# A retuned stage of routing gates in a one-layer decoder kernel: buffers, order numbers and four early rows

## The chip, the cores and the metric

The kernel runs on one core of one Trainium2 chip. Its time is the device time of one execution in microseconds (us). The median of the three runs shown is 1644.31 us (1640.9 to 1646.19). The profiled execution took 1639.83 us; the time from its first to its last instruction, the span, is 1638.0 us. All times of the trace count from the span's start.

## The reference

One inference step of a one-layer decoder on 544 tokens (512 of a prompt, 8 sequences of 4), 1024 wide, fp32. The first half (a mixer with pooling and mLSTM heads) is finished before the part that changes. The second half is PEER, a product-key retrieval over 16384 experts of one neuron each:

```
def one(xb):                                             # a block of tokens
    q = (xb @ w_q).reshape(blk, PEER_HEADS, 2, HALF_KEY)
    s = jnp.einsum('nhpc,hpkc->nhpk', q, keys)
    sv, si = lax.top_k(s, TOPK)                          # 8 heads, 2 halves, 16 of 128 keys
    comb = sv[:, :, 0, :, None] + sv[:, :, 1, None, :]
    cidx = si[:, :, 0, :, None] * N_KEYS + si[:, :, 1, None, :]
    top, sel = lax.top_k(comb.reshape(..., 256), TOPK)
    eidx = jnp.take_along_axis(cidx.reshape(..., 256), sel, axis=-1)
    g = jax.nn.softmax(top, axis=-1)
    act = jax.nn.gelu(jnp.einsum('nd,nhkd->nhk', xb, u_tab[eidx]), approximate=False)
    return jnp.einsum('nhk,nhkd->nd', g * act, v_tab[eidx])
```

Each token uses 128 rows of u_tab and of v_tab (8 heads of 16).

## The kernel before

Tokens stand in five tiles: 0 to 3 of the prompt, 128 tokens each, and 4, the 32 sampled tokens. Two ways to compute PEER run side by side.

Tiles 1 to 3 (384 tokens) take the dense way, in 128 blocks of 128 experts. A **u block** (`uphase`) multiplies 128 rows of u_tab with all 384 tokens on TensorE: 24 matmuls of 384 columns into the bank pH, then one GELU on ScalarE into a tile act. Each factor is split into a high and a low part, so that three products replace an fp32 one: ScalarE writes the high part whi of a loaded weight tile raw, and VectorE or GpSimd the **low part** wlo = raw - whi. The first 16 matmuls of a u block need whi, the last 8 wlo. A **v block** (`vprep`, `ymm`) multiplies act by the block's gates (tile gr), splits the result into chi and clo, splits 128 rows of v_tab (tile vr), and adds 18 matmuls of 512 columns into the six banks Y. Activations of the first `AHEAD - RING` blocks are parked in DRAM (Ad) and reloaded as tile ar; the later ones stay in a ring of RING tiles.

Tiles 0 and 4 take the gathered way (`gathered`): for each of 160 steps (128 and 32) GpSimd's queue issues an indirect DMA that fetches one row of u_tab per token (128 rows of 4 KB), VectorE makes the dot product with the token (the tile dot), and then the same with v_tab rows, weighted and summed into y2. The rows pass through eight buffers rbuf, which share memory with the two halves of the tile stage.

The gates of the dense way are made in between. `topks` runs on VectorE tile by tile: the expert indices of the 16 chosen (tile f) by 16-fold one-hot products (eq, tr), and the softmax weights g. For tiles 1 to 3, three transposes on TensorE turn f and g. Then `gates_of` makes the gate rows, 8 tokens at a time, a **group**, 48 in all: VectorE writes a one-hot tile E and a tile P in two halves, TensorE multiplies them in 16 matmuls into two banks pg, ScalarE copies these into stage, and every four groups stage is written to DRAM (Gd), from which v blocks read their gates. GB is the number of buffers of P; E has one more.

All engines run in the order in which the program is written (a manual schedule). Where u blocks, top-k pieces and groups interleave is set by a small model while the program is built: the loop below `side, more, b, held = topks(), ...`. It keeps two clocks in us, `pe` and `dve`. Each piece of top-k yields its VectorE time, a group costs GRP there and PEG on TensorE, a u block PEU on TensorE and its low part LOU on VectorE; VectorE's clock starts at TOFF, the offset to TensorE's first u block after the sort. A group is placed on TensorE once its clock says that it is ready, else the next u block is. The first PLO low parts after the four that are placed earlier go to GpSimd, all later ones to VectorE. `WI.deep` is the number of blocks whose parts are written ahead of the one in use: the parts of block n + deep stand in the queues of ScalarE and VectorE before the GELU of block n. Of weight tiles (raw and vr together) four are in memory at a time.

When the groups are placed, RES u blocks remain before the passage to v blocks. In it SP's queue issues, in this order, the reloads of act (ar), the gates of the first four v blocks (gr), the remaining weight tiles and the first v rows; each waits for its buffer. The gathered steps start in the last three u blocks, GPRE steps in each, with up to seven rows fetched ahead (`Ahead`, depth 7). The first coefficient's low part clo is on GpSimd, behind the gathers issued so far. Then the loop over v blocks runs: while b is below AHEAD - RING it has v blocks alone with GV gathered steps each, then one u block and one v block an iteration with `pace` steps, at last v blocks alone.

Of the kernel before, what the change touches and what calls it, by code (L numbers as in the profile page):

```python
# [8 lines left out]
F32 = mybir.dt.float32  # L9
# [25 lines left out]
NRAW = 4  # L35
NSP = 4
GORD = (3, 2, 1, 0)
AHEAD = 55
SPILL = AHEAD - RING
GB = 5  # L40
RES = 6
GPRE = 2
GRP = 2.65
LOU = 1.25
LOL = 2.50
PLO = 4
PEU = 4.25
PEG = 1.10
TOFF = 14.00
PEW = 0.50  # L50
LEAD = 4.00
PRE = (4, 7, 10, 13)
# [94 lines left out]
def body(tc, a, o, stop=None):  # L147
# [1083 lines left out]
    eid = {0: gat.tile([128, 128], I32, name="eid0"), 4: gat.tile([128, 32], I32, name="eid4")}  # L1231
    gcf = {0: gat.tile([128, 128], F32, name="gcf0"), 4: gat.tile([128, 32], F32, name="gcf4")}
    nstep = {0: 128, 4: 32}
    heads_of = [slice(8 * t, 8 * t + 8) for t in range(4)] + [slice(32, 34)]

    def ranks():
        ex = grl.tile([128, HS, 16], F32, name="ex")
        tmp = keep.tile([128, 6, HS, 16], F32, name="rtmp", tag="ylo")
        ri, ci, cf_, rf, t1, t2 = (tmp[:, k] for k in range(6))
        ri, ci = ri.bitcast(I32), ci.bitcast(I32)  # L1240
        nc.vector.tensor_tensor(ex, top, top[:, :, 0:1].to_broadcast([128, HS, 16]), op=ALU.subtract)
        hk = "q h k -> q k h"
        si = sel.bitcast(I32)
        nc.vector.tensor_scalar(ri, si, 3, None, op0=ALU.arith_shift_right)
        nc.vector.tensor_copy(rf, ri)
        nc.vector.tensor_scalar(ci, si, 7, None, op0=ALU.bitwise_and)
        nc.vector.tensor_copy(cf_, ci)
        yield 3.0
# [9 lines left out]
        yield 5.5  # L1258
        return ex, sx, ii, jj

    def exps(ex):
# [6 lines left out]
    def topk(t, ex, sx, ii, jj):  # L1268
# [10 lines left out]
        for p, src in ((0, ii), (1, jj)):  # L1279
            eq = grl.tile([128, 16 * K], F16, name="eq", tag="eq", bufs=1)  # L1280
            e4 = eq.rearrange("q (b k h) -> q b k h", b=16, k=16)
            nc.vector.tensor_tensor(e4, src[:, None, :, hs].to_broadcast([128, 16, 16, nh]),
                                    io16[:, :, 0:K].rearrange(v, k=16), op=ALU.is_equal)
            nc.vector.tensor_tensor(e4, e4, ib[:, p, None, :, :].rearrange("q o b h -> q b o h").to_broadcast([128, 16, 16, nh]),
                                    op=ALU.mult)
            tr = grl.tile([128, 8 * K], F16, name="tr", tag="tr", bufs=1)
            nc.vector.tensor_tensor(tr, eq[:, 0:8 * K], eq[:, 8 * K:], op=ALU.add)
            for w in (4, 2):
                nc.vector.tensor_tensor(tr[:, 0:w * K], tr[:, 0:w * K], tr[:, w * K:2 * w * K], op=ALU.add)
            nc.vector.tensor_tensor(f[:, p, :], tr[:, 0:K], tr[:, K:2 * K], op=ALU.add)  # L1290
            if t == TORD[0] and p:
                sums(ex, sx)
            yield 4.2 if K == 128 else 1.6
# [4 lines left out]
        if t in eid:  # L1298
            nc.vector.scalar_tensor_tensor(eid[t], f[:, 0, :], 128.0, f[:, 1, :], op0=ALU.mult, op1=ALU.add)
        else:  # L1300
            turned.append((t, f, g))

    GSC = 2.0 ** 15
    stage = [None]
# [18 lines left out]
    def gates_of(ring):  # L1323
# [28 lines left out]

        todo = [(t, n0) for t in (1, 2, 3) for n0 in range(0, 128, W)]
        E = one_hot(*todo[0])
        for j, (t, n0) in enumerate(todo):
            nE = one_hot(*todo[j + 1]) if j + 1 < len(todo) else None
            P = ring.tile([128, 2, R, 128, RUN], F16, name="P", tag="P", bufs=GB)
            for k in (1, 0):
# [5 lines left out]
    def topks():  # L1364
# [3 lines left out]
        for t in TORD:  # L1368
# [1 line left out]
            for _ in last:  # L1370
                pass
            if turned:
                yield 1.6
                last = gates_in()
                yield next(last)
                next(last)
# [5 lines left out]
        yield from gates_of(ring)  # L1382


    WI.deep = 3
    side, more, b, held = topks(), True, next(nu), False
    pe, dve, wait, freed, lo_at = 0.0, TOFF, [], [], [0.0] * PLO
    while more or wait:
# [13 lines left out]
        elif b < AHEAD - RES and not (wait and wait[0][0] <= pe + PEW):  # L1402
# [2 lines left out]
            b += 1  # L1405
            pe = max(pe, lo_at.pop(0) - LOL) + PEU
            if b + WI.deep > ub + PLO:
                dve = max(dve, pe - PEU) + LOU
                lo_at.append(dve + 0.2)
        else:  # L1410
            ready, run_it = wait.pop(0)
            run_it()
            pe = max(pe, ready) + PEG
            freed.append(pe + 0.2)
    WI.deep = 2
    grx.close()
    gpx.close()
    gs.close()
# [5 lines left out]
    utab, vtab = a["u_tab"], a["v_tab"]  # L1424
    rbuf = [keep.tile([128, 4, D], F32, name="rbuf", tag=k) for k in ("yhi", "ylo")]
    rn = [0]

    def gathered():
        for t in (0, 4):
            n = nstep[t]  # L1430
            u = utok if t == 0 else usam
            dots = vp.tile([128, n], F32, name=f"dot{t}")
            cf = vp.tile([128, n], F32, name=f"cf{t}")
            CH = 16

            def row_of(tab, k):
                g = rbuf[rn[0] % 8 // 4][:, rn[0] % 4, :]
                rn[0] += 1
                nc.gpsimd.indirect_dma_start(out=g, out_offset=None, in_=tab,  # L1439
                                             in_offset=bass.IndirectOffsetOnAxis(ap=eid[t][:, k:k + 1], axis=0))  # L1440
                return g
            work = [("u", k) for k in range(CH)]
            for c0 in range(0, n, CH):
                work += [("c", c0)]
                for k in range(c0, c0 + CH):
                    work += [("v", k)] + ([("u", k + CH)] if k + CH < n else [])
            seq = [w for w in work if w[0] != "c"]
            q = Ahead(lambda i: row_of(utab if seq[i][0] == "u" else vtab, seq[i][1]), len(seq), 7)
            for kind, k in work:
                if kind == "u":  # L1450
                    g = q.get()
                    nc.vector.scalar_tensor_tensor(g, g, 1.0, u, op0=ALU.mult, op1=ALU.mult,  # L1452
                                                   accum_out=dots[:, k:k + 1])
                    yield 1
                elif kind == "c":
                    s = slice(k, k + CH)
                    nc.scalar.activation(cf[:, s], dots[:, s], AF.Gelu)
# [152 lines left out]
    while todo_u < AHEAD:  # L1610
# [6 lines left out]
            vprep(2 - AHEAD + todo_u)  # L1617
        uphase(todo_u)
        todo_u += 1
    done = 3 * GPRE  # L1620
    spent = float(done)
    pace = (320 + 1 - done - GV * (AHEAD - RING) - GV2 * (RING - GEND)) / (NB - AHEAD)
    ends, early = None, 0
    for b in range(NB - 1):
        if todo_u < NB and todo_u - b <= RING:
# [12 lines left out]
        if b < NB - LASTB:  # L1638
            for t in range(NDT):
                ymm(b, t)  # L1640
        want = min(320, int(spent))
        steps(gg, want - done)
        done = want
        if todo_u == NB and done >= 264 and FWAIT in fin and ends is None:
# [109 lines left out]
```

## Time and profile before

| | |
|---|---|
| median of 3 runs | 1644.31 us (1640.9 to 1646.19) |
| profiled execution | 1639.83 us, span 1638.0 us |
| TensorE busy (PE, matmuls) | 1548.3 us, 95% |
| VectorE busy (DVE) | 1349.4 us, 82% |
| ScalarE busy (ACT) | 639.6 us, 39% |
| GpSimd busy (POOL) | 698.2 us, 43% |
| bytes moved by DMA | 454.93 MB, mean 278 GB/s |

PE is TensorE, DVE VectorE, ACT ScalarE, POOL GpSimd, SP the engine that issues loads; SPq, ACTq and POOLq are their DMA issues. PEclk is the clock that TensorE was granted, 1.00 being 2.4 GHz and half of it 1.2 GHz. A span on GpSimd is rough. Matmuls overlap: one that is listed with 0.34 us starts 0.17 us after the one before it, so distances between starts are read, not durations. The part that the change touches lies between about 500 and 950 us: top-k to 591, groups to 738, the passage, and v blocks alone to 948. The rows below are of that part.

### The profile page before, as it was taken

The page shows a single profiled execution, that of the slowest core. Times are in us where ns is not written, and L with a number is a line of the kernel's source. Part 1 is how long each engine was busy: PE and PEld are TensorE (multiplying, and loading weights), DVE is VectorE, ACT ScalarE, POOL GpSimd, SP SyncE. Part 2 cuts the span into 40 slices and gives each one's busy share as a digit, 9 for nine tenths or more (in the row PEclk, how much of TensorE's full clock was granted, in tenths as well). Part 3 has the DMA queues.
Part 4 walks back from the last instruction along what each step waited for, and adds up shares of the span by engine and source line. Part 5 has one row for each costly group of instructions (what it writes and reads, how often), then busy time and mean ns, then how long its engine had stood idle before and what let it go on. Part 6 is the DMA issues. An engine that isn't in the chain of part 4 may idle for free.

```text
span 1638.0 us, 25202 instructions
## 1 busy us (share of the span) xinstructions
PE 1548.3 (95%) x9293; PEld 1378.1 (84%) x9293; DVE 1349.4 (82%) x2737; ACT 639.6 (39%) x999; POOL 698.2 (43%) x518
## 2 busy tenths in 40 slices
PE   5999998896999999998999999999999999999994
PEld 3888886676999989998788799999999999999873
DVE  6634468698999899994788789899889898989986
ACT  4322223555534345563333333333333333333343
POOL 2433333466551000004233356656565665566615
PEclk9999999998999999999999999999999999999997
DMA  9544456544344548769999989999999999999981
GB/s 346 179 145 155 151 150 186 196 170 132 111 142 151 186 165 290 283 267 350 374 369 381 357 311 378 378 367 369 367 379 381 353 370 376 375 366 367 388 282 68
DMA packets 180847, 454.93 MB, mean 278 GB/s; under 512 B 23216, under 2 KB 84016, under 8 KB 179060
## 3 DMA queue, kind: packets, MB, share of 16 engines
q1 hardware_dynamic: 119736, 246.70, 44.1%
q0 software_dynamic: 46080, 167.79, 27.0%
q10 hardware_dynamic: 14908, 38.84, 6.2%
q8 instruction: 73, 1.20, 0.3%
q14 instruction: 50, 0.41, 0.1%
HBM read 412.74 MB, written 40.53 MB: 277 GB/s over the span
## 4 chain that ended last, share of the span: by engine, by line
PE 72%; DVE 14%; DMA 7%; ACT 3%; issue 2%; POOL 1%; SPq 0%; ACTq 0%; DVEq 0%; POOLq 0%
PE pH L162 29%; PE Y L162 24%; PE bk L162 10%; PE tb L162 4%; DMA gr<-Gd 3%; PE pg L162 3%; DVE wlo L447 2%; PE pm L162 1%; DMA vr<-in_v_tab_dram 1%; DMA wm<-in_w_mod_r_dram 1%; PE tb L166 1%; DMA rbuf<-in_u_tab_dram,eid 1%; DVE ost L251 1%; ACT whi L445 1%; DVE x L987 1%
## 5 line engine op out<-in xcount | busy, mean ns | idle before, releaser
L1439 POOL DMA_INDIRECT rbuf<-in_u_tab_dram,eid x160 | 212.1, 1326 | 424.3 <-ACT stage L1347 235.4
L162 PE MATMUL pH<-u2hi,whi 128*128 128x384 f32 x992 | 338.1, 341 | 0.8 <-ACT act L1194 0.8
L162 PE MATMUL pH<-u2lo,whi 128*128 128x384 f32 x992 | 335.2, 338 | 0.0
L1439 POOL DMA_INDIRECT rbuf<-in_v_tab_dram,eid x160 | 237.0, 1481 | 178.2 <-DVE y L1464 125.5
L445 ACT ACTIVATE whi<-raw 128x1024 fp32r<-128x1024 f32 (+1 forms) x193 | 202.8, 1054 | 143.6 <-issue 96.5
L445 ACT ACTIVATE whi<-vr 128x1024 fp32r<-128x1024 f32 x128 | 135.6, 1059 | 300.5 <-PE Y L162 233.0
L162 PE MATMUL Y<-whi,chi 128*128 128x512 f32 x768 | 240.7, 392 | 5.4 <-ACT chi L1505 5.4
L162 PE MATMUL Y<-whi,clo 128*128 128x512 f32 x768 | 241.0, 393 | 2.3 <-DVE clo L1506 1.2
L162 PE MATMUL Y<-wlo,chi 128*128 128x512 f32 x768 | 239.4, 390 | 0.0
L447 POOL TENSOR_TENSOR wlo<-raw,whi 128x1024 fp32r<-128x1024 f32 (+2 forms) x65 | 152.0, 2347 | 160.3 <-ACT whi L445 158.9
L447 DVE TENSOR_TENSOR wlo<-vr,whi 128x1024 fp32r<-128x1024 f32 x128 | 156.6, 1223 | 75.8 <-ACT whi L445 69.0
L1464 DVE SCALAR_TENSOR_TENSOR y<-rbuf,cf,y 128x1024 f32<-128x1024 f32 x158 | 202.7, 1283 | 0.9
L162 PE MATMUL pH<-u2hi,wlo 128*128 128x384 f32 x992 | 194.4, 337 | 0.0
L162 PEld LDWEIGHTS pH<-u2hi,whi 128*128 128x128 f32 x992 | 186.9, 188 | 4.1 <-ACT act L1194 1.1
L162 PEld LDWEIGHTS pH<-u2lo,whi 128*128 128x128 f32 x992 | 186.9, 188 | 2.8
L447 DVE TENSOR_TENSOR wlo<-raw,whi 128x1024 fp32r<-128x1024 f32 (+1 forms) x132 | 160.3, 1217 | 34.0 <-ACT whi L445 25.3
L162 PEld LDWEIGHTS pH<-u2hi,wlo 128*128 128x128 f32 x992 | 175.8, 188 | 0.0
L162 PEld LDWEIGHTS Y<-whi,clo 128*128 128x128 f32 x768 | 144.2, 189 | 36.6 <-DVE clo L1506 5.0
L162 PEld LDWEIGHTS Y<-whi,chi 128*128 128x128 f32 x768 | 143.4, 188 | 32.9 <-ACT chi L1505 7.0
L162 PEld LDWEIGHTS Y<-wlo,chi 128*128 128x128 f32 x768 | 144.9, 189 | 30.4
L1452 DVE SCALAR_TENSOR_TENSOR rbuf<-rbuf,utok 128x1024 f32<-128x1024 f32 x128 | 156.0, 1221 | 1.6 <-DMA rbuf<-in_u_tab_dram,eid 1.6
L1194 ACT ACTIVATE act<-pH 128x384 f32<-128x384 f32 x124 | 60.8, 490 | 132.6 <-PE pH L162 128.7
(402 smaller groups left out, 2401.7 us busy)
## 6 DMA issues: line engine op xcount, KB each, us to landing
raw<-in_u_b_dram SPq DMA_DIRECT2D x128, 512.0 KB
vr<-in_v_tab_dram SPq DMA_DIRECT2D x128, 512.0 KB
wm<-in_w_mod_r_dram SPq DMA_DIRECT2D x48, 512.0 KB
gr<-Gd SPq DMA_DIRECT2D x32, 768.0 KB
Gd<-stage ACTq DMA_DIRECT2D x9, 2048.0 KB
raw<-in_w_q_b_dram SPq DMA_DIRECT2D x32, 512.0 KB
raw<-in_w_in_b_dram SPq DMA_DIRECT2D x20, 512.0 KB
Ad<-act ACTq DMA_DIRECT2D x42, 192.0 KB
```

The lines of the kernel that those rows point to most:

```text
L162: nc.tensor.matmul(out, l, r, start=start, stop=stop, skip_group_check=True)
L166: nc.tensor.transpose(out, x, idn)
L251: nc.vector.bn_stats(st[:, i, :], x[:, 512 * i:512 * (i + 1)])
L445: nc.scalar.activation(hi, raw, AF.Copy)
L447: e.tensor_tensor(lo[:, d], raw[:, d], f32(hi[:, d]), op=ALU.subtract)
L987: e.tensor_tensor(x1[:, d], x1[:, d], l1b[:rows, d], op=ALU.add)
L1194: nc.scalar.activation(x, p[:, 0:ND], AF.Gelu)
L1439: nc.gpsimd.indirect_dma_start(out=g, out_offset=None, in_=tab, in_offset=bass.IndirectOffsetOnAxis(ap=eid[t][:, k:k + 1], axis=0))
L1452: nc.vector.scalar_tensor_tensor(g, g, 1.0, u, op0=ALU.mult, op1=ALU.mult, accum_out=dots[:, k:k + 1])
L1464: nc.vector.scalar_tensor_tensor(y2[t], g, cf[:, k:k + 1], y2[t], op0=ALU.mult, op1=ALU.add)
```

## The change

Constants: P has three buffers instead of five (GB) and E four instead of six; the memory holds four row tiles re instead. Six low parts go to GpSimd instead of four (PLO). 53 u blocks are placed ahead of the loop over v blocks instead of 55 (AHEAD), so 40 activations are parked instead of 42. One gathered step in each of the last three u blocks instead of two (GPRE). The model's costs are new (GRP, LOU, TOFF and the times that top-k's pieces yield), and it now reckons a low part's earliest start one u block earlier. `WI.deep` stays 2 all the time, where it was 3 during top-k and groups. The first four u rows of tile 0 are gathered into the tiles re at a place of the program between the groups, and their dots follow the last group; the gathered steps then begin with row 4, at first with four rows ahead instead of seven.

```
-AHEAD = 55
+AHEAD = 53
-GB = 5
+GB = 3
+EG = 4
-GPRE = 2
-GRP = 2.65
-LOU = 1.25
+GPRE = 1
+GRP = 2.40
+LOU = 1.15
-PLO = 4
+PLO = 6
-TOFF = 14.00
+TOFF = 19.00
...
+    def gather(g, tab, t, k):
+        nc.gpsimd.indirect_dma_start(out=g, out_offset=None, in_=tab,
+                                     in_offset=bass.IndirectOffsetOnAxis(ap=eid[t][:, k:k + 1], axis=0))
+        return g
+
+    def dot_u(g, t, k):
+        nc.vector.scalar_tensor_tensor(g, g, 1.0, utok if t == 0 else usam, op0=ALU.mult, op1=ALU.mult,
+                                       accum_out=dots[t][:, k:k + 1])
...
+            if (t, n0) == (3, 32):
+                for k in range(EG):
+                    rows_early.append(gather(ring.tile([128, D], F32, name="re", tag="re", bufs=EG), utab, 0, k))
...
-    WI.deep = 3
     side, more, b, held = topks(), True, next(nu), False
...
             if b + WI.deep > ub + PLO:
-                dve = max(dve, pe - PEU) + LOU
+                dve = max(dve, pe - 2 * PEU) + LOU
                 lo_at.append(dve + 0.2)
...
-    WI.deep = 2
+    for k, g in enumerate(rows_early):
+        dot_u(g, 0, k)
...
-            work = [("u", k) for k in range(CH)]
+            work = [("u", k) for k in range(len(rows_early) if t == 0 else 0, CH)]
...
+            if t == 0:
+                rowq.append(q)
+                q.depth = 4
...
+    rowq[0].depth = 7
-    done = 3 * GPRE
+    done, ngat = 3 * GPRE, 320 - EG
     spent = float(done)
-    pace = (320 + 1 - done - GV * (AHEAD - RING) - GV2 * (RING - GEND)) / (NB - AHEAD)
+    pace = (ngat + 1 - done - GV * (AHEAD - RING) - GV2 * (RING - GEND)) / (NB - AHEAD)
```

How the instructions move. On TensorE the u blocks between the sets of transposes and the first group were 11, 3, 4 and 4 and are now 11, 4, 3 and 5; between the 48 groups stood 23 u blocks, two groups after almost each, and now stand 20, with two or three groups in turn.

On VectorE, where top-k ends (gcf and eid are its last tiles) and the groups begin. Before:

```order
L447 TENSOR_TENSOR wlo<-raw,whi 128x1024
L1295 TENSOR_TENSOR gcf_5575<-ex,sx_5735 128x2x16
L1299 SCALAR_TENSOR_TENSOR eid_5573<-f_6361 128x32
L1332 TENSOR_TENSOR E<-iT_4392,io_4391 128x2048 x2
L1360 TENSOR_TENSOR P<-E,gp_4395 128x1024 x2
L1332 TENSOR_TENSOR E<-iT_4392,io_4391 128x2048
```

Now:

```order
L1298 TENSOR_TENSOR gcf_5575<-ex,sx_5765 128x2x16
L1302 SCALAR_TENSOR_TENSOR eid_5573<-f_6391 128x32
L1346 TENSOR_TENSOR E<-iT_4392,io_4391 128x2048
L448 TENSOR_TENSOR wlo<-raw,whi 128x1024
L1346 TENSOR_TENSOR E<-iT_4392,io_4391 128x2048
L1378 TENSOR_TENSOR P<-E,gp_4395 128x1024 x2
```

A low part stands between the first two E; from the start of top-k (the tile ex) to the first E there are 17 low parts, where 20 stood, and 21 instead of 23 between the first and the last E.

On GpSimd, from its last low parts to the first v rows of the gathered way. Before:

```order
L447 TENSOR_TENSOR wlo<-raw,whi 128x1024 x22
L1439 DMA rbuf<-in_u_tab_dram,eid_5572 128x1024 x10
L1506 TENSOR_TENSOR clo<-ar,chi 128x384
L1439 DMA rbuf<-in_u_tab_dram,eid_5572 128x1024 x6
L1439 DMA rbuf<-in_v_tab_dram,eid_5572 128x1024
```

Now:

```order
L448 TENSOR_TENSOR wlo<-raw,whi 128x1024 x24
L1309 DMA re<-in_u_tab_dram,eid_5572 128x1024 x4
L1309 DMA rbuf<-in_u_tab_dram,eid_5572 128x1024 x5
L1523 TENSOR_TENSOR clo<-ar,chi 128x384
L1309 DMA rbuf<-in_u_tab_dram,eid_5572 128x1024 x7
L1309 DMA rbuf<-in_v_tab_dram,eid_5572 128x1024
```

Ten gathers stood ahead of the first clo, now nine do, of which the four into re wait for nothing but the indices (eid); seven instead of six follow it.

On SP, the loads at the passage. Before:

```order
L420 DMA raw<-in_u_b_dram 128x1024 x50
L1491 DMA ar<-Ad 128x384 x5
L1477 DMA gr<-Gd 128x12x128
L420 DMA raw<-in_u_b_dram 128x1024 x3
L1483 DMA vr<-in_v_tab_dram 128x1024 x4
```

Now:

```order
L421 DMA raw<-in_u_b_dram 128x1024 x47
L1508 DMA ar<-Ad 128x384 x5
L421 DMA raw<-in_u_b_dram 128x1024
L1494 DMA gr<-Gd 128x12x128
L421 DMA raw<-in_u_b_dram 128x1024 x3
L1500 DMA vr<-in_v_tab_dram 128x1024 x4
```

One weight tile, that of the fifth of the last six u blocks, now stands behind the reloads ar.

## Rows read from the trace of the kernel before

**Rows 1.** Stretches: us, then each engine's busy us and instructions, PEclk, DMA share, GB/s.
```profile
560.00:590.00 30.00, 30.00 (x175) 29.96 (x174) 27.21 (x53) 10.88 (x14) 0.00 (x0) 1.00 0.47 147
...
738.40:767.90 29.50, 25.51 (x144) 24.86 (x143) 9.29 (x13) 7.07 (x12) 10.18 (x10) 1.00 1.02 376
...
790.60:944.00 153.40, 152.13 (x664) 124.26 (x665) 130.38 (x184) 57.60 (x77) 50.72 (x44) 1.00 1.03 368
...
944.00:1550.60 606.60, 606.60 (x3068) 554.59 (x3068) 541.40 (x682) 221.16 (x299) 370.36 (x253) 1.00 1.00 369
```
**Rows 2.** Chain of waits, 480 to 860 us: start us, us, what.
```profile
496.94 46.47 PE pH L162 x264
...
595.83 5.40 PE pH L162 x24
...
603.08 4.26 PE pH L162 x24
...
607.35 1.85 PE pg L162 x32
```
**Rows 3.** Chain of waits, 860 to 1638 us.
```profile
948.29 4.22 PE pH L162 x24
...
952.50 4.09 PE Y L162 x18
```
**Rows 4.** TensorE timeline: start us, us, what, [idle before it <- who ended it].
```profile
594.33 1.50 PE L162 MATMUL pg<-P,E 128*128 128x128 f16 x16 [3.65 <-DVE P L1360]
...
767.90 0.73 PE L162 MATMUL Y<-whi,chi 128*128 128x512 f32 x2 [3.22 <-ACT chi L1505]
...
769.60 1.22 PE L162 MATMUL Y<-whi,clo 128*128 128x512 f32 x2 [0.96 <-POOL clo L1506]
...
775.72 0.62 PE L162 MATMUL Y<-wlo,chi 128*128 128x512 f32 x2
...
789.64 0.73 PE L162 MATMUL Y<-whi,chi 128*128 128x512 f32 x2 [1.06 <-ACT chi L1505]
```
**Rows 5.** VectorE timeline, top-k and gate products.
```profile
502.19 1.23 DVE L1120 TENSOR_TENSOR scr<-scr 128x32 f32<-128x32 f32 x1
...
510.26 0.17 DVE L1120 TENSOR_TENSOR scr<-scr 128x32 f32<-128x32 f32 x1
...
541.31 1.23 DVE L447 TENSOR_TENSOR wlo<-raw,whi 128x1024 fp32r<-128x1024 f32 x1 [1.49 <-ACT whi L445]
...
571.40 1.22 DVE L447 TENSOR_TENSOR wlo<-raw,whi 128x1024 fp32r<-128x1024 f32 x1 [1.79 <-ACT whi L445]
...
590.72 2.35 DVE L1332 TENSOR_TENSOR E<-iT,io 128x2048 f16<-128x2048 f16 x2
...
727.80 1.22 DVE L447 TENSOR_TENSOR wlo<-raw,whi 128x1024 fp32r<-128x1024 f32 x1
728.94 1.22 DVE L1332 TENSOR_TENSOR E<-iT,io 128x2048 f16<-128x2048 f16 x1
730.08 1.28 DVE L1360 TENSOR_TENSOR P<-E,gp 128x1024 f16<-128x1024 f16 x2
731.28 1.21 DVE L1332 TENSOR_TENSOR E<-iT,io 128x2048 f16<-128x2048 f16 x1
```
**Rows 6.** ScalarE, then GpSimd timeline.
```profile
758.72 1.06 ACT L445 ACTIVATE whi<-raw 128x1024 fp32r<-128x1024 f32 x1 [7.17 <-DMA raw<-in_u_b_dram]
...
766.38 1.06 ACT L445 ACTIVATE whi<-vr 128x1024 fp32r<-128x1024 f32 x1 [6.22 <-DMA vr<-in_v_tab_dram]
...
498.60 4.78 POOL L447 TENSOR_TENSOR wlo<-raw,whi 128x1024 fp32r<-128x1024 f32 x2 [3.29 <-ACT whi L445]
...
738.74 1.16 POOL L1439 DMA_INDIRECT rbuf<-in_u_tab_dram,eid  x1 [235.36 <-ACT stage L1347]
...
752.85 1.53 POOL L1439 DMA_INDIRECT rbuf<-in_u_tab_dram,eid  x1 [9.23 <-DMA Gd<-stage]
```

More of the change, by code (lines that the diff above doesn't have):

```diff
@@ L1233, in body @@
     nstep = {0: 128, 4: 32}
+    dots = {0: gat.tile([128, 128], F32, name="dot0"), 4: gat.tile([128, 32], F32, name="dot4")}
+    rows_early = []
     heads_of = [slice(8 * t, 8 * t + 8) for t in range(4)] + [slice(32, 34)]
@@ L1247, in ranks @@
         nc.vector.tensor_copy(cf_, ci)
-        yield 3.0
+        yield 2.4
         ii = grl.tile([128, 16, HS], F16, name="ii")
@@ L1257, in ranks @@
         sx = grl.tile([128, HS], F32, name="sx2")
-        yield 5.5
+        yield 4.5
         return ex, sx, ii, jj
@@ L1292, in topk @@
                 sums(ex, sx)
-            yield 4.2 if K == 128 else 1.6
+            yield (4.5 + 0.4 * (1 - p) + (1.1 if t == TORD[0] and p else 0.0)) if K == 128 else 2.1
         g = gcf[t] if t in gcf else grl.tile([128, 128], F32, name="g", tag="g", bufs=2)
@@ L1301, in topk @@
             turned.append((t, f, g))
+    utab, vtab = a["u_tab"], a["v_tab"]
+    def gather(g, tab, t, k):
[5 more added lines that the diff above has]
+                                       accum_out=dots[t][:, k:k + 1])
     GSC = 2.0 ** 15
@@ L1354, in gates_of @@
         E = one_hot(*todo[0])
+        yield 1.2
         for j, (t, n0) in enumerate(todo):
+            if (t, n0) == (3, 32):
+                for k in range(EG):
+                    rows_early.append(gather(ring.tile([128, D], F32, name="re", tag="re", bufs=EG), utab, 0, k))
             nE = one_hot(*todo[j + 1]) if j + 1 < len(todo) else None
@@ L1372, in topks @@
             if turned:
-                yield 1.6
+                yield 1.0
                 last = gates_in()
@@ L1423, in body @@
     y2 = {t: vp.tile([128, D], F32, name=f"y2_{t}") for t in (0, 4)}
-    utab, vtab = a["u_tab"], a["v_tab"]
+    rowq = []
     rbuf = [keep.tile([128, 4, D], F32, name="rbuf", tag=k) for k in ("yhi", "ylo")]
@@ L1430, in gathered @@
             n = nstep[t]
-            u = utok if t == 0 else usam
-            dots = vp.tile([128, n], F32, name=f"dot{t}")
+            dot = dots[t]
             cf = vp.tile([128, n], F32, name=f"cf{t}")
@@ L1438, in row_of @@
                 rn[0] += 1
-                nc.gpsimd.indirect_dma_start(out=g, out_offset=None, in_=tab,
-                                             in_offset=bass.IndirectOffsetOnAxis(ap=eid[t][:, k:k + 1], axis=0))
-                return g
-            work = [("u", k) for k in range(CH)]
+                return gather(g, tab, t, k)
+            work = [("u", k) for k in range(len(rows_early) if t == 0 else 0, CH)]
             for c0 in range(0, n, CH):
@@ L1451, in gathered @@
                     g = q.get()
-                    nc.vector.scalar_tensor_tensor(g, g, 1.0, u, op0=ALU.mult, op1=ALU.mult,
-                                                   accum_out=dots[:, k:k + 1])
+                    dot_u(g, t, k)
                     yield 1
@@ L1456, in gathered @@
                     s = slice(k, k + CH)
-                    nc.scalar.activation(cf[:, s], dots[:, s], AF.Gelu)
+                    nc.scalar.activation(cf[:, s], dot[:, s], AF.Gelu)
                     nc.vector.tensor_tensor(cf[:, s], cf[:, s], gcf[t][:, s], op=ALU.mult)
@@ L1640, in body @@
                 ymm(b, t)
-        want = min(320, int(spent))
+        want = min(ngat, int(spent))
         steps(gg, want - done)
         done = want
-        if todo_u == NB and done >= 264 and FWAIT in fin and ends is None:
+        if todo_u == NB and done >= 264 - EG and FWAIT in fin and ends is None:
             nc.scalar.preload_act_table_set("natural_log_exp_and_others")
```

## The prediction

> **What bounds the kernel now.** I read the page's slices first, then a table of stretches, the chain of waits from 480 us on, and last the timelines of the engines where TensorE has gaps. TensorE is the bound: from 944 to 1551 us it is busy in every one of 606.6 us [rows 1], and the chain there is one u block of 4.22 us and one v block of 4.09 us in turn [rows 3]. No edit takes a product away, so time can come only from TensorE's gaps near the change. There are two places. At the first gate products TensorE waits 3.65 us for VectorE and the next u block takes 5.40 us instead of 4.26 [rows 2, 4]. At the passage from u blocks to v blocks it waits 3.22, 0.96 and 1.06 us, and the eight pairs of v products from 767.90 to 775.72 take 6.86 us beside the 0.96, where eight pairs at 4.09/9 take 3.64: 3.2 us lost at half clock [rows 3, 4]. I call 738.4 us, where the last gate products end, G: 594.33 + 1.50 + 5.40 + 22 u blocks at 4.26 + 47 groups at 0.925 (half of 1.85) [rows 2, 4]. From G the kernel has six u blocks (25.3 us) and 42 v blocks (171.8) until the loop's first u block at 948.29 [rows 3]; ideal would be 935.5, so the passage loses 12.8 us. All through it the DMA engines are full: 376, then 368 GB/s [rows 1].
>
> **Top-k on VectorE, up to the first gate products.** A group on VectorE costs 1.14 us for the one-hot E and 1.20 for both halves of P, a low part 1.14, each the distance between two starts [rows 5]. By the order, 17 low parts stand there instead of 20: -3.4 us (two went to GpSimd, one more comes later because two blocks are prepared ahead instead of three). That same line costs something: the low part of block n now follows the GELU of block n-3, not n-4, so it cannot start until TensorE has ended n-3 and about 1.5 us have passed on ScalarE. Walking down the order with TensorE at 4.22 us a block (46.47/11 [rows 2]) I get four waits of 0.4, 0.6, 3.05 and 2.7 us, against 1.49 and 1.79 before [rows 5]: +3.5. The first E stays at 590.8 (before 590.72 [rows 5]). But TensorE now has 23 u blocks ahead of the first gates instead of 22 and arrives at 496.94 + 23 x 4.22 + 1.0 for three sets of transposes = 595.0. The first group is ready after E, a low part, E and P: 590.8 + 3 x 1.14 + 1.20 = 595.4. The wait falls from 3.65 us to about 0.4, too short for the clock to fall: after the wait of 1.06 us at 789.64 the granted clock was 1.00 [rows 1, 4].
>
> GpSimd's two extra low parts are not free for VectorE. A 128x32 addition took 1.23 us at 502.19, until GpSimd's low parts were over, and 0.17 us at 510.26 with GpSimd idle [rows 5, 6]. Two more low parts there (2.39 us each, half of 4.78) could hold VectorE up to 4.8 us where they save 2.3. The Trainium skill, "SBUF — State Buffer", section "Who interferes with whom", says the two engines share a port pair that one of them locks for a whole instruction when a Vector instruction has two SBUF inputs; by it the edit would lose up to 2.5 us of VectorE, and the trace agrees (1.23 against 0.17 us). In the sum I take 0: GpSimd gets these blocks' high parts at about 507 and 511 us, and the waits of 3 us later in top-k, which TensorE's pace sets, swallow the delay. If nothing swallows it, the first E is 2.5 us late.
>
> **The gate stage.** With the new order 20 u blocks stand between 48 groups, by twos and threes, where 23 stood before. TensorE: 48 x 0.925 + 20 x 4.26 = 129.6 us. VectorE: 48 x 2.34 + 21 x 1.14 = 136.3 us. So VectorE becomes the bound: it ends at 590.8 + 136.3 = 727.1, the last products 0.93 later, 728.0 at the earliest. TensorE meets the third group of a triple before it is ready, nine times by 0.6 to 0.9 us; walking down the order, G comes at 729.0 to 730.4. I take 729.5. Two u blocks are still owed at this point: 2 x 4.21 = 8.4, so 737.9 against 738.4: **-0.5 us**, with ends of -2 (G at 728.0) and +3.5 (first E 2.5 late and another 1.5 lost). Three buffers instead of five let VectorE run three groups ahead; in the walk no E or P waits for a buffer.
>
> **The passage.** Before, ten gathers (0.52 MB each) were issued here ahead of the first coefficient's low part, four from G on and six from 752.85 on, when the last stage write landed [rows 6]. Behind them the loads starved: the sixth u block's weights were waited for until 758.72, the first v rows until 766.38 [rows 6], 28 us after G. Now four rows are fetched earlier (by the order they need only the indices, so from about 584 us on, beside a DMA share of 0.47 [rows 1]) and five gathers, not ten, stand ahead of that low part. That is 2.6 MB, or 7 us at 376 GB/s, less in front of the first v rows. Against it, the first load of the six blocks that used to go out earlier (the fifth) now stands behind the five reloads: 0.5 MB, 1.4 us. The dots of the four early rows (4 x 1.22 = 4.9 us on VectorE) lie beside u blocks whose low parts are needed only at G + 11 us: no cost. So the first v rows land at about G + 22 to 24 instead of G + 27.9, and TensorE's own u blocks, ending at G + 25.3, come last, with 0.7 us left for ScalarE's high part and coefficients and about 1.1 for GpSimd's low part. Gained: 3.22 - 0.7 = 2.5, and the 3.2 us of half clock if waits of 0.7 and 1.1 us leave the clock up: 5.7; some of the rest (1.06 at 789.64, later waits) goes too.
> A second way to the same term: in this phase DMA is as full as TensorE. Until the loop's first u block it now moves two v blocks less (0.52 + 0.2 + 0.2 MB each) and 5.4 gathers less (3 + 40 x 1.2 against 6 + 42 x 1.2 rows), 4.7 MB or 12.6 us at 370 GB/s, while TensorE has 8.2 us less to do there: 4.4 us of slack, and up to 2 more because the first gathers wait for a stage write that now goes out 4 us earlier before G. Bounds: 0 (the loads stay as late, relative to the u blocks) and -10 (only unavoidable waits stay). I take **-6.5 us**, near what the two ways give.
>
> **The rest.** 128 u blocks and 128 v blocks remain; the loop takes 3.42 rows an iteration against 3.49 (the pace line), so DMA has a little less to do in a stretch where TensorE waits for nothing. At the end the order differs by one row sum moved one block: 0 +- 0.5.
>
> **Sum.** -0.5 - 6.5 = -7.0 us on the profiled execution's 1639.83 us (span 1638.0): 1632.8. That execution is 4.5 us under the median of the three runs; on the median the same step gives 1644.31 - 7.0 = 1637.3.
>
> **Rivals.**
> (a) The gate stage takes back what the passage gives. VectorE is the bound there, and each 0.1 us on a group is 4.8 us; with the +3.5 end and only -3 at the passage the change is +0.5: 1644.8. For it: 136.3 against 129.6 us. Against: the wait of 3.65 us that goes was larger.
> (b) Slower: three buffers are too few. If in each of the 20 rounds P waits for a buffer that TensorE frees late, VectorE, the bound, never makes it up: at 0.7 us a round G is 14 us later, -0.5 + 14 - 6.5 = +7.0: 1651. It decides from 0.6 us a round on. For it: the groups now come in threes, the number of buffers. Against: during a u block of 4.26 us VectorE makes a low part and 1.3 groups, and three may be open.
> (c) The transfer is no earlier. The fifth of the six blocks, now loaded behind the reloads, lands as late as the sixth did (G + 20.3): TensorE waits 4.5 us for it at G + 16.8 and loses 3.2 at half clock, v blocks begin at G + 33.0, which against G + 29.5 plus 0.96 and 3.2 lost there is -0.7; with the gate term -1: 1643.
> (d) More than forecast: the passage gives -10 and the gates -2: 1632.
>
> **How the numbers follow.** Chances: the forecast 0.50, its own range 1633 to 1641; (d) 0.10; (a) 0.15; (c) 0.15; (b) 0.10. About 0.3% (4.9 us) is the least that a measurement of this kernel tells from no change. Faster by more: most of the forecast and (d), 0.54. Slower by more: (b) and a little of (a), 0.12. Same: 0.34. The range takes in (a), (c) and (d), and a scatter of the runs of 2 to 3 us: 1629 to 1646.
>
> **What would show it.** Right: TensorE's wait before the first gate products under 1 us; then several waits on P of under 1 us each and the last gate products near 729.5 us; early gathers on GpSimd near 584 us; the first v product about 26 us after G with no half clock behind it. Wrong: G after 733 us, P waiting on TensorE, a wait for the fifth block's load, or the first v product 29 us after G again.

## The result, and the profile after

The changed kernel takes 1658.09 us (median of five runs, 1655.38 to 1660.94); the kernel before, run beside it, 1646.19 (1640.9 to 1651.18). The ratio is 1.0073, 95% interval 1.0045 to 1.0101: 12 us slower, where 7 us faster was forecast and the range ended at 1646. The profiled execution is the one of 1658.09 us, span 1655.9 against 1638.0.

The gate stage went as forecast. The chain of the kernel after (start, us, what), the timeline of GpSimd, and that of TensorE with idle time and its releaser in brackets:

```profile
502.46 46.48 PE pH L163 x264
...
596.82 1.22 DVE E L1346
```
```profile
590.76 1.16 POOL L1309 DMA_INDIRECT re<-in_u_tab_dram,eid  x1 [70.96 <-DVE eid L1302]
```
```profile
601.57 1.08 PE L163 MATMUL pg<-P,E 128*128 128x128 f16 x16 [1.15 <-DVE P L1378]
...
733.93 2.01 PE L163 MATMUL pg<-P,E 128*128 128x128 f16 x32
```

The u blocks begin 5.5 us later than in [rows 2], before any line that the change touches; the same start lies at 501.9, 502.0 and 503.2 us in three profiled variants of the kernel before (e3, e8, e2 below). That is scatter, and I subtract it. From the first u block to the last gate products are 233.5 us (733.93 + 2.01 - 502.46) against 241.5; with two u blocks owed (8.4) the stage costs 0.5 us more than before, where -0.5 was forecast.

What the prediction said of GpSimd's two extra low parts shows too. GpSimd, then VectorE beside them:

```profile
513.20 2.40 POOL L448 TENSOR_TENSOR wlo<-raw,whi 128x1024 fp32r<-128x1024 f32 x1 [1.80 <-ACT whi L446]
517.41 2.40 POOL L448 TENSOR_TENSOR wlo<-raw,whi 128x1024 fp32r<-128x1024 f32 x1 [1.80 <-ACT whi L446]
```
```profile
514.72 0.93 DVE L1121 TENSOR_TENSOR scr<-scr 128x32 f32<-128x32 f32 x1
...
517.81 2.58 DVE L1244 TENSOR_TENSOR ex<-top 128x544 f32<-128x544 f32 x1
```

The first addition takes 0.17 us with GpSimd idle [rows 5], the second took 0.72 us in the kernel before: together 2.6 us lost on VectorE, where the kernel before lost 1.1 on one addition [rows 5]. The first E is only 0.5 us later than forecast, so the later waits swallowed most of it, as the sum had assumed.

The passage did not go as forecast. TensorE, ScalarE, VectorE and SyncE's DMA issues of the kernel after:

```profile
756.24 0.69 PE L163 MATMUL pH<-u2hi,whi 128*128 128x384 f32 x1 [3.42 <-ACT act L1195]
...
766.16 0.63 PE L163 MATMUL Y<-whi,chi 128*128 128x512 f32 x2
...
790.14 1.22 PE L163 MATMUL Y<-whi,chi 128*128 128x512 f32 x2 [6.49 <-ACT chi L1522]
```
```profile
754.76 1.06 ACT L446 ACTIVATE whi<-raw 128x1024 fp32r<-128x1024 f32 x1 [9.82 <-DMA raw<-in_u_b_dram]
...
763.70 1.06 ACT L446 ACTIVATE whi<-vr 128x1024 fp32r<-128x1024 f32 x1 [2.31 <-DMA vr<-in_v_tab_dram]
```
```profile
788.91 0.56 DVE L1519 TENSOR_TENSOR ar<-ar,gr 128x384 f32<-128x384 f32 x1 [10.11 <-DMA gr<-Gd]
```
```profile
735.97 2.54 SPq L1508 DMA_DIRECT2D ar<-Ad  x5
738.61 0.66 SPq L421 DMA_DIRECT2D raw<-in_u_b_dram  x1
744.21 0.37 SPq L1494 DMA_DIRECT2D gr<-Gd  x1
750.19 2.67 SPq L421 DMA_DIRECT2D raw<-in_u_b_dram  x3
757.10 11.23 SPq L1500 DMA_DIRECT2D vr<-in_v_tab_dram  x4
...
772.76 0.44 SPq L1494 DMA_DIRECT2D gr<-Gd  x1
```

The chain has the links between these rows, and the last line is that of the kernel before:

```profile
738.61 16.06 DMA raw<-in_u_b_dram
...
755.85 1.24 DVE wlo L448
757.10 6.52 DMA vr<-in_v_tab_dram
```
```profile
753.13 13.17 DMA vr<-in_v_tab_dram
```

The fifth u block's weights are issued behind the five reloads and land 16 us later, at 754.7. The first v rows wait for the load buffer that this block holds: they go out at 757.1, when its low part is done, and ScalarE takes them at 763.7. Counted from the last gate products (G), they go out at 21.2 us instead of 14.7, but are under way for 6.5 us instead of 13.2. The second gate rows (issued at 772.8) arrive at 788.9; around their issue GpSimd sends out seven gathers in a row. The last gather ahead of them, then the first and the last of the seven:

```profile
750.96 0.94 POOL L1309 DMA_INDIRECT rbuf<-in_u_tab_dram,eid  x1 [10.05 <-issue]
...
767.05 1.75 POOL L1309 DMA_INDIRECT rbuf<-in_u_tab_dram,eid  x1 [0.15 <-issue]
...
777.16 1.30 POOL L1309 DMA_INDIRECT rbuf<-in_u_tab_dram,eid  x1 [0.30 <-issue]
```

The table of stretches (us, busy us and instructions of PE, PEld, DVE, ACT, POOL, granted clock, DMA share, GB/s) shows what the transfers did meanwhile:

```profile
736.00:746.00 10.00, 10.00 (x59) 10.00 (x59) 5.21 (x8) 3.66 (x6) 4.00 (x4) 1.00 0.92 322
746.00:756.00 10.00, 6.82 (x39) 6.50 (x38) 0.15 (x1) 1.24 (x2) 0.94 (x1) 1.00 1.05 378
756.00:766.00 10.00, 9.76 (x48) 9.76 (x49) 6.26 (x8) 3.93 (x6) 0.74 (x1) 0.83 0.71 265
766.00:800.00 34.00, 27.35 (x110) 21.00 (x109) 22.77 (x34) 11.01 (x17) 13.45 (x12) 0.90 0.97 338
...
943.50:1550.00 606.50, 606.50 (x3038) 550.17 (x3037) 528.17 (x664) 219.98 (x297) 363.12 (x245) 1.00 0.99 360
```

Before, the engines moved 376 GB/s over these 30 us [rows 1] (335, 382 and 408 in three stretches of about 10); now they fall to 265 just when the v rows are due. Little has been issued that they could move: SyncE's queue issues nothing from 752.9 to 757.1, and GpSimd no gather from 751.9 to 767.05. And the last row holds the surprise: from 943.5 to 1550 us TensorE waits for nothing and its clock is whole, as in [rows 1], yet the DMA engines move 360 GB/s, not 369: everything runs slower. The chain says why:

```profile
943.62 4.22 PE pH L163 x24
947.84 4.17 PE Y L163 x18
```

A v block takes 4.17 us, not 4.09 [rows 3]. The mean distances between the starts of its 18 products (59 or 60 blocks from 1000 to 1500 us, ns):

```
before 232 231 227 227 227 227 227 227 227 227 227 227 227 227 227 227 227 227  sum 4090
after  232 228 230 233 241 232 231 232 228 230 233 241 233 231 232 228 230 227  sum 4170
```

Every block repeats its pattern, at the whole clock and without a wait; in the kernel after the distances recur every seven products. What differs is where operands lie. The row dots moved into the pool gat (640 bytes more in each partition), before everything that is allocated later, and out of the pool of the coefficients (512 bytes less ahead of them), so the coefficient tiles chi and clo now start 128 bytes later: at 64 bytes past a multiple of 256, before at 192 past one (all eight alike). The tiles whi and wlo, which stream past them, stay at 192.

The difference of the spans, stage by stage: start +5.5 (scatter); gate stage +0.5; from the last gate products to the loop's first u block 207.7 us against 209.9, with two v blocks (8.2) fewer, +6.0; 74 pairs of the loop at 0.086 us, +6.4; the end -0.5. Sum 17.9. These are one execution of each kernel. From the last gate products to the loop, other profiled executions of the old order took 209.2 us (e8 below) and, with slower v blocks, 213.0, 213.3 and 215.5 (e2, e3, e10), so the +6.0 is uncertain by some us; what the runs say of it stands with e1.

### The profile page after: what moved, and what is told of

The parts are those of the page before. It is cut to its first block, busy times and chain, and to the rows that moved or that the text cites. A ratio compares the mean times of both kernels' runs of the same rounds, so it can differ in the third digit from the quotient of the medians.

```text
span 1655.9 us, 25195 instructions
## 1 busy us (share of the span) xinstructions
PE 1565.8 (95%) x9293; PEld 1385.2 (84%) x9293; DVE 1348.0 (81%) x2735; ACT 638.7 (39%) x999; POOL 709.1 (43%) x520
## 4 chain that ended last, share of the span: by engine, by line
PE 67%; DVE 20%; DMA 6%; issue 3%; ACT 2%; POOL 1%; SPq 0%; ACTq 0%; DVEq 0%; POOLq 0%
PE Y L163 27%; PE pH L163 23%; PE bk L163 10%; PE tb L163 4%; DMA gr<-Gd 3%; DVE E L1346 3%; DVE wlo L448 3%; DVE P L1378 3%; DMA raw<-in_u_b_dram 1%; PE pm L163 1%; DMA wm<-in_w_mod_r_dram 1%; PE tb L167 1%; DVE ost L252 1%; DVE x L988 1%; ACT whi L446 1%
## 5 line engine op out<-in xcount | busy, mean ns | idle before, releaser
L163 PE MATMUL Y<-wlo,chi 128*128 128x512 f32 x768 | 243.9, 396 | 0.0
L448 POOL TENSOR_TENSOR wlo<-raw,whi 128x1024 fp32r<-128x1024 f32 (+2 forms) x67 | 157.0, 2352 | 163.7 <-ACT whi L446 162.3
L1314 DVE SCALAR_TENSOR_TENSOR rbuf<-rbuf,utok 128x1024 f32<-128x1024 f32 x124 | 151.2, 1220 | 0.0
```

What stands on the lines that cost most here:

```text
L163: nc.tensor.matmul(out, l, r, start=start, stop=stop, skip_group_check=True)
L448: e.tensor_tensor(lo[:, d], raw[:, d], f32(hi[:, d]), op=ALU.subtract)
L1314: nc.vector.scalar_tensor_tensor(g, g, 1.0, utok if t == 0 else usam, op0=ALU.mult, op1=ALU.mult, accum_out=dots[t][:, k:k + 1])
```

## Experiments: where the operands lie

**e1 and e2: the coefficient tiles moved, the order left as it is.**

```
-            cf = vp.tile([128, n], F32, name=f"cf{t}")
+            cf = vp.tile([128, n + 96], F32, name=f"cf{t}")[:, 0:n]     e1, of the kernel after
+            cf = vp.tile([128, n + 32], F32, name=f"cf{t}")[:, 0:n]     e2, of the kernel before
```


> The changed kernel, with the tile cf0 made 384 bytes longer a partition, so that the coefficient tiles chi and clo behind it start 384 bytes later: at 448 bytes past a multiple of 512 again, as in the kernel before (the change put them at 64 past one). Nothing else moves. Theory A (where the coefficient tiles lie sets the rate of the v products): a v block takes 4.09 us again instead of 4.17, 128 x 0.08 = 10 us less, about 1648. Theory B (the rate comes from the order: 53 blocks ahead, other buffers for v rows, gathers at other moments): v blocks stay at 4.17 and the time at 1658.

> The kernel before, with the tile cf0 made 128 bytes longer, so that chi and clo lie where the changed kernel has them (64 bytes past a multiple of 512). Order and everything else as before. Theory A: v blocks of 4.17 us instead of 4.09, about 1656, 10 us slower than before. Theory B: 4.09 and no change, 1646.

Measured: e1 1649.19 us, ratio to before 1.0003 (0.9985 to 1.0022); e2 1655.16, 1.0046 (1.0028 to 1.0065). The chains of e1 and of e2:

```profile
1404.98 4.09 PE Y L163 x18
```
```profile
1406.63 4.17 PE Y L162 x18
```

Theory A holds in both directions, B falls: the same order with the tiles moved back has the old rate, and the old order with the tiles moved has the new one, within a nanosecond (e2 repeats the pattern of "after" above). In e1's profile the loop is 6.4 us shorter than in the kernel after, the stretch ahead of it only 0.4. There the 40 faster v blocks wait for transfers instead: from the first v product to the loop e1 takes 176.9 us, where 40 x 4.09 are 163.6. By the runs, what the change does besides moving the tiles is worth +0.5 us (ratio 1.0003, -2.5 to +3.6 us), where -7.0 was forecast.

In e1 and e2 all that is allocated behind cf0 moves along, not the coefficients alone. e3 below settles that: there the time of a block follows the place of its own chi and clo.

**e3, e8, e10: other places.**

```
-        ch, cl = (vp.tile([128, ND], F32R, name="c" + k, tag="c" + k, bufs=CB) for k in ("hi", "lo"))
+        ch, cl = (vp.tile([128, ND + 16], F32R, ..., bufs=CB)[:, 0:ND] for k in ("hi", "lo"))     e3
+    keep.tile([128, 16], F32, name="padw")        e8, ahead of wst; cf0 longer by 192 bytes
+    hi, lo = (wst.tile([128, D + 16], F32R, name=k, tag=k, bufs=NSP)[:, 0:D] ...)                 e10
```


> The kernel before with each buffer of chi and of clo made 64 bytes longer (not used), so that the four buffers start at different places: chi at 448, 0, 64 and 128 bytes past a multiple of 512, clo at 192, 256, 320 and 384. Theory A: the v blocks no longer take one time; every fourth block has its own, between 4.0 and 4.2 us, and the block whose chi starts at 64 is slower than the one at 448. Theory B: all v blocks take 4.09.

> The kernel before with all load and split buffers (raw, whi, wlo) 64 bytes later, so that whi and wlo start at a multiple of 256 instead of 192 past one, and the coefficients kept at 192 past one. In v products whi and wlo stream past and the coefficients are the stationary operand; in u products whi and wlo are the stationary operand. Theory H (the place of the stationary operand alone decides): v blocks 4.09 us, and u blocks slower than 4.22. Theory I (the two operands' places against each other decide): v blocks at 4.20, like the pair 64 bytes apart the other way round, or at 4.13.

> The kernel before with each buffer of whi and wlo made 64 bytes longer (not used), so that the four start at 192, 0, 64 and 128 bytes past a multiple of 256, the coefficients kept at 192. By turns v blocks then have whi and wlo at 192 and 64, u blocks at 0 and 128. From e3 and e8: v blocks 4.09 with whi at 192 and 4.12 at 0, u blocks 4.22 at 192 and 4.19 at 0. Theory H (the stationary operand's place alone decides) fell with e8's v blocks. Theory J (each operand's place has its own price, and the prices add up): v blocks with whi at 64 take 4.15 to 4.18, u blocks at 0 take 4.19, and u blocks at 128 another time, 4.17 to 4.25. Theory I (only the distance of the two operands): v blocks with whi at 64 (coefficients 128 further) take 4.17, as in e3 with the coefficients 128 off.

The chains of e3, e8 and e10 in the loop, of one execution each:

```profile
1412.55 4.09 PE Y L162 x18
...
1420.86 4.13 PE Y L162 x18
...
1429.21 4.17 PE Y L162 x18
...
1437.60 4.20 PE Y L162 x18
```
```profile
1401.12 4.19 PE pH L162 x24
1405.32 4.12 PE Y L162 x18
```
```profile
1405.03 4.20 PE Y L162 x18
1409.23 4.20 PE pH L162 x24
1413.43 4.09 PE Y L162 x18
1417.52 4.19 PE pH L162 x24
```

In bytes past a multiple of 256, with e11 below (in e3 chi and clo of one block stand at the same place by this count):

```
whi, wlo  chi, clo   v block   u block
192       192        4.09      4.22     before, e1
192         0        4.13               e3
192        64        4.17      4.22     after, e2, e3
192       128        4.20               e3
  0       192        4.12      4.19     e8
 64       192        4.20               e10
128         -                  4.20     e10
  0         0        4.10      4.20     e11
```

Theory A's forecast for e3 holds: four times, in turn. H falls with e8: the coefficients stood where they are fast, and the v block still rose from 4.09 to 4.12. J and I each miss a row: J (prices add) forecast 4.15 to 4.18 for whi at 64 and 4.16 for e11; I (distance alone) would give 192/128 and 0/192, both 64 bytes apart by the same way round, one time, and they have 4.20 and 4.12. What is shown is that the places of both operands count, at 64-byte steps, by up to 2.6% of a block, and that the best of those tried has both at the same place. The place of whi alone does not set the u block either: with whi at 0 it has 4.19 in e8 and 4.20 in e11. Why stays open. The Trainium skill, "SBUF — State Buffer", section "Specifications (TRN2)", speaks of lines of 16 bytes; by it places that are all multiples of 64 would be alike, and here they are not (4.09 to 4.20 us).

## Experiments: the passage

**e4, e5, e6, e7: one hold-up taken away at a time**, all with e1's coefficient tiles.

```
+    WI.early = 3                     e4: the fifth u block's load ahead of the reloads
+    WI.load()
     aq.fill()
-GV = 1.20
+GV = 1.10                            e5: e4, and fewer rows beside v blocks alone
+        if AHEAD - todo_u == 2:      e6: e4, and the second gate rows ahead of the v rows
+            load_g(4)
-        if b % 4 == 0 and b:
+        if b % 4 == 0 and b > 4:
         if AHEAD - todo_u == 5:
+            vq.depth = 1             e7: e4, and the first v rows in a buffer of their own
+            vq.fill()
+            vq.depth = 3
-        r = wst.tile([128, D], F32, name="vr", tag="raw", bufs=NRAW)
+        r = (wst.tile([128, D], F32, name="vr", tag="raw", bufs=NRAW) if b else
+             vp.tile([128, D], F32, name="vr", tag="sq", bufs=1))
```


> The kernel of e1_after_shift, and besides the fifth of the last six u blocks has its weights' load issued before the five reloads of activations, as in the kernel before. Theory C (the passage lost its gain because that load stood behind the reloads): ScalarE's wait of 9.8 us for it and TensorE's of 3.4 us go, the v blocks begin 3 us earlier, and the time is 3 us under e1_after_shift's. Theory D (the DMA queues are full there, so that what is loaded earlier makes another load later, first the v rows or the second gate rows gr, for which TensorE waits 6.5 us): the wait of 3.4 us goes but later ones grow, and the time is within 1 us of e1_after_shift's.

> The kernel of e4_fifth_load_first with 1.1 gathered rows instead of 1.2 beside each v block that has no u block (40 of them; the four rows, 2.1 MB, come later, in the loop). Theory E (from the last gate products to the loop's first u block the kernel is bound by what the DMA engines move; 371 GB/s in e4 from 800 to 936 us): 2.1 MB at 371 GB/s is 5.7 us that the v blocks get, as far as TensorE waits or runs at half clock there (e4 needs 175.5 us from the first v product to the loop's first u block, where 40 x 4.09 are 163.6): u1 - v0 of 170 to 172 and 1643 to 1645. Theory F (TensorE waits there for single late transfers, not for the amount): no change, 1648; or slower, if the loop, where the DMA engines are at 0.99, cannot take four rows more.

> The kernel of e4_fifth_load_first with the second load of gate rows (gr for v blocks 4 to 7) issued ahead of the first v rows instead of behind the fifth. Theory F (a single late transfer): the wait for gr at the fifth v block (3.6 us in e4, 6.5 in the changed kernel, each with half clock behind it) goes, u1 - v0 falls from 175.5 to about 170, 1643 to 1645. Theory E (amount): another wait takes its place, and u1 - v0 stays within 1.5 us, 1648.

> The kernel of e4_fifth_load_first with the first v rows in a buffer of their own, loaded right behind the fifth u block's weights, instead of in one of the four load buffers that the u blocks still hold (in e4 the first v rows are issued at 752.3 us, 19 us after the last gate products, and the DMA engines are at 206 GB/s from 753 to 763). Theory G (the load buffers, not the DMA engines, hold the first v rows back, and the engines idle meanwhile): the first v product comes at once behind the u blocks, 25.3 to 26.5 us after the last gate products instead of 27.95, the engines move 300 GB/s or more all through, and the time falls by 2 to 5 us, to 1643 to 1646. Rival: later waits take it back, 1648.

Measured (v0 is the first v product's start behind the last gate products; then from v0 to the loop's first u block):

```
      time us   ratio to before (95%)       v0      to the loop
e1    1649.19   1.0003 (0.9985, 1.0022)     30.2    176.9
e4    1648.23   1.0005 (0.9989, 1.0021)     28.0    175.5
e5    1648.44   1.0008 (0.9991, 1.0026)     29.3    173.5
e6    1648.33   1.0004 (0.9987, 1.0021)     31.9    173.7
e7    1645.82   0.9991 (0.9971, 1.0012)     25.1    175.8
```

None can be told from before by its time; the times of 1643 to 1645 that E and F forecast for e5 and e6 did not come, e7's lies in G's range but not clear of noise. The profiles show why, TensorE's timeline of e4, of e6 and of e7:

```profile
761.31 0.73 PE L163 MATMUL Y<-whi,chi 128*128 128x512 f32 x2 [2.65 <-ACT chi L1522]
...
785.56 0.73 PE L163 MATMUL Y<-whi,chi 128*128 128x512 f32 x2 [3.58 <-ACT chi L1522]
```
```profile
767.74 1.22 PE L163 MATMUL Y<-whi,chi 128*128 128x512 f32 x2 [6.63 <-ACT chi L1522]
```
```profile
788.24 1.22 PE L163 MATMUL Y<-whi,chi 128*128 128x512 f32 x2 [4.99 <-ACT chi L1523]
```

In e4 the wait of 3.4 us for the fifth block is gone (C), but the first v rows and gr are waited for, as D said, and the engines fall to 206 GB/s from 753.4 to 763.4 us. The edit does more than put the fifth load back: with WI.early at 3, one weight tile more than in the kernel after goes out ahead of the first v rows (56 instead of 55), and these now wait for the buffer of the sixth block. The chain of e4:

```profile
735.78 14.08 DMA raw<-in_u_b_dram
...
751.04 1.24 DVE wlo L448
752.29 7.41 DMA vr<-in_v_tab_dram
```

So the v rows go out at G + 18.9 in e4 and at G + 21.3 in e5, not at 14.7 as in the kernel before; what the fifth load alone costs no run shows. In e6 the wait for gr is gone (F), but behind the load that now stands ahead of them the first v rows are under way for 9.2 us (7.4 in e4, 6.4 in e5), and v0 is 3.9 us later than in e4, 2.6 later than in e5. In e7 the first v product comes at once (G, whose 300 GB/s are nearly reached: 317, 385, 298 in three stretches of 10 us), and gr is waited for. In e5 the forecast of E, 170 to 172, is missed by 1.5 us, and v0 is later. Up to v0 e4 and e5 have the same loads, so 28.0 and 29.3 also show how far two executions differ. Each edit hands the wait to the next transfer in line.

**e9: e5, e6 and e7 together.** The lines of all three, as above.

> The kernel of e7_first_v_own_buffer with the edits of e5_fewer_rows (1.1 rows) and e6_second_gate_rows_early. In e7 the first v product comes at 25.1 us behind the last gate products, but the fifth v block waits 5.0 us for gr and u1 - v0 is 175.8 us; e5 and e6 had 173.5 to 173.7. Theory E and F together (amount and a single late transfer): u1 - v0 falls to 168 to 170, the first v product stays at 25 to 27 us, about 6 us under e7, 1639 to 1641 where before is at 1647. Rival (the DMA engines are full from 776 us on, so what is taken away in one place is given back in another): u1 - v0 of 173 or more, 1644 to 1646.

Measured: 1637.23 us, ratio 0.9932 (0.9908 to 0.9955); v0 at 25.1, then 168.9 us. TensorE's timeline of e9 has one wait of some size left, and the engines stay full where they fell before (stretches as above):

```profile
766.76 0.73 PE L163 MATMUL Y<-whi,chi 128*128 128x512 f32 x2 [2.77 <-ACT chi L1523]
```
```profile
755.00:765.00 10.00, 8.99 (x46) 7.93 (x45) 4.54 (x6) 1.96 (x3) 5.42 (x5) 1.00 1.08 366
```

E and F hold together: 11 us under e4, more than the sum of the three alone (2.4, 0 and 0). 1639 to 1641 was forecast beside 1647 for the kernel before, which took 1648.2 here. Whether two of the three would do was not tried. This version is faster than both kernels.

**e11 and e12: the best of both, and the passage without the change.** e11 is e9 with e8's line padw alone, so that all four tiles start at a multiple of 256; e12 is the kernel before with the three edits of e9.

> The kernel of e9_passage_together with all load, split and coefficient buffers 64 bytes later: whi, wlo, chi and clo all start at a multiple of 256. Measured so far: whi at 192 with coefficients at 0: v block 4.13; whi at 0 with coefficients at 192: 4.12; whi at 0: u block 4.19 instead of 4.22. Theory J (the two prices add up): v blocks of 4.16, 128 x 0.07 slower, less 124 x 0.026 for the u blocks: 5 to 6 us slower than e9, about 1643. Theory I (only the distance of the two counts): v blocks of 4.09 again, and the u blocks' 3.2 us are gained: about 1634.

> The kernel before, with the three edits of the passage that e9_passage_together has (1.1 rows instead of 1.2 beside a v block without a u block, the second gate rows ahead of the first v rows, the first v rows in a buffer of their own), but without the change itself: five buffers of gate rows, no early rows, ten gathers ahead of the first coefficient, 55 blocks ahead. Theory K (the change gives what was forecast, once its loads are not held up): this comes out 4 to 7 us over e9, 1642 to 1644. Theory L (the change's own part is worth nothing, the three edits are all): the same as e9, 1637 to 1639. Rival: with ten gathers ahead, the first v rows stay late and the edits give nothing, 1647.

Measured: e11 1635.71 us, 0.9939 (0.9918 to 0.996): no difference from e9. Its chain:

```profile
1403.80 4.10 PE Y L163 x18
1407.90 4.20 PE pH L163 x24
```

J falls (v blocks 4.10, not 4.16), and I's gain on the u blocks is half what it was in e8 (4.20). e12 1642.81, 0.9978 (0.996 to 0.9995): within K's forecast, 5.6 us over e9 by the medians and 7.6 by the ratios; the two intervals do not meet, but they leave the size open by some 5 us either way. L falls; the rival's 1647 too. e12's profile is of its slowest execution (1652.93 us, 10 over the median). In it the weights of the sixth of the last u blocks, issued among the ten gathers, land 24 us later, and TensorE waits 11.2 us for them, a wait that e9 does not have:

```profile
758.29 23.94 DMA raw<-in_u_b_dram
```

From the first v product on it loses nothing (171.8 us to the loop, 42 x 4.09). If its other executions lose the same there, this is where the change's fewer gathers pay; no profile of one shows it.

## Why the prediction was wrong

1. **The step that failed first is one that the sum did not have.** "No edit takes a product away, so time can come only from TensorE's gaps" and "The rest ... 0 +- 0.5" took 4.22 and 4.09 us a block as fixed. The v block became 4.17. Worth 6.4 us in the loop by the profiles; in all 8.9 us by the medians of e1 and the kernel after, 11.5 by their ratios. No view of before shows it; the addresses of the two programs would have shown that the tiles move, not what that costs.
2. **The passage, -6.5 us, gave nothing.** It was +6.0 by the two profiles; by the runs, gate stage and passage together are +0.5 us (e1, -2.5 to +3.6), so how far beyond nothing it went is not known. The failed sentence is "the first load of the six blocks ... now stands behind the five reloads: 0.5 MB, 1.4 us". I priced the load's own bytes. It landed 16 us after its issue, and the first v rows stood behind it, not only in the DMA queue but for its load buffer, so they went out 6.4 us later (G + 21.2 against 14.7). Against that they were under way for 6.5 us instead of 13.2, which fits the 7 us forecast for five gathers fewer, though no run takes these away alone. The two cancel. "The first v rows land at about G + 22 to 24": ScalarE took them at G + 27.8, before at G + 28.0 [rows 6]. e7 shows the link of the buffer: with a buffer of their own v0 is 25.1 instead of 30.2, where 26 was forecast. e4 shows that TensorE's wait goes when the load goes out earlier, and no more, since its v rows stand behind the sixth block instead. This is rival (c), given 0.15, with its wait (4.5 forecast, 3.42 measured); its price for gate and passage, -1 us, lies within e1's interval. The wait for the fifth block and the first v product 29 us after G (30.2) are two of the prediction's own signs of being wrong.
3. **The second way to the same term** counted 12.6 us of DMA time less and assumed that the engines stay full. They fell to 265 GB/s: SyncE stood at a load whose buffer was not free, GpSimd at the first coefficient, and the gathers that used to fill this stretch were gone.
4. **The wait of 6.49 us for gr was not foreseen.** Seven gathers now go out in a row behind the first coefficient's low part, around gr's issue, where six stood; before, TensorE's wait at that place was 1.06 us [rows 4]. That the gathers make gr late is argued, no run changes them alone; issuing gr earlier (e6 and e9) takes the wait away.
5. **What held.** The first E at 591.3 us less the scatter (590.8 forecast); the first gate products after a wait of 1.15 us (0.4 forecast, 3.65 before); early gathers at 585.3 less the scatter (584); three buffers are enough, so rival (b) falls: VectorE waits for no buffer of E or P, and the last gate products come at 730.4 less the scatter (729.5), not 14 us later. The two low parts on GpSimd cost VectorE 2.6 us, of which 0.5 at most reached the first E.
6. **The size of the idea may be right, its sum was not.** With the loads freed and the coefficients at the old place, the change is worth 5.6 to 7.6 us (e9 against e12); 7.0 was forecast. But both have three edits that the forecast did not know, and e9 has the fifth block's load ahead of the reloads again: that the number fits is partly luck.

## What to carry to other kernels

Compare the addresses of TensorE's operands when a change adds or moves a tile, even a small one that no product reads: a block whose products all take a little longer, without a wait and at full clock, points there. Before moving a load behind others, ask not what its bytes cost but which buffer it fills, and what is issued only when that buffer comes free. Ask apart when a transfer is issued and how long it is under way: here the first became 6.4 us later and the second 6.7 us shorter, and nothing was gained. Where a chain of transfers is late, removing one wait may show nothing in the time until the next ones go too, as in e5 and e6, so try the edits together before dropping them.

## What was not expected of the hardware

The 128x512 products of a v block have starts 227 ns apart (but for the first two of a block, 232 and 231) where stationary and moving operand both start 192 bytes past a multiple of 256, and 228 to 241 ns, in a pattern that repeats every seven products, with the stationary one moved on by 128 bytes. Over a block that is 4.09 against 4.17 us, and 4.20 at the worst place tried; the 128x384 products of a u block range from 4.19 to 4.22. The same pattern returned in every block of the loop and in two different kernels (the kernel after and e2).
